# Output products of a diffusion block: from float32 pairs to scaled float16 pairs

## The chip, the cores and the metric

One core of one Trainium2 chip runs the whole kernel in one launch. The metric is the device time of one execution in microseconds. Before the change three runs took 2703.93, 2701.36 and 2702.88 us (median 2702.88).

## What is computed

The reference is one block of a diffusion transformer over 2048 tokens of width 1024, in float32. The input projection and the gates are followed by a Fourier mixer (512 channels) and by a neighbourhood attention (8 heads of 64) side by side. Their outputs are merged, projected and added to the stream, and an MLP follows. What the change touches is the merge:

```python
def gated_merge(h, y_four, y_attn, w_gate, w_fo, w_ao, w_o):
    gates = jax.nn.sigmoid(h @ w_gate)
    g_f, g_a = jnp.split(gates, N_BRANCHES, axis=-1)
    merged = g_f * (y_four @ w_fo) + g_a * (y_attn @ w_ao)
    return merged @ w_o
...
    x = x + g1 * mixed
```

Here `y_attn` is 2048x512, `w_ao` 512x1024, `w_o` 1024x1024.

## The kernel before

Precise products are made from pairs. A float32 tile is split into a high part and the rest (`split_on`, L85: ACT copies the high part, L87, another engine subtracts, L90), and `mm3` (L76) issues three matmuls per pair of operands, high x high, high x low, low x high, all on line L82. Some products take float16 pairs whose operands are scaled beforehand (the projections `ps_*`, the MLP products `pm` and `p`). Others, among them the two of this change, take pairs of type float32r, a 4-byte type.

The stages, in order of time in the profiled execution:

- To 850 us: norm, modulation and projections in pairs of weight units. The last pair is two gate units, g6 and g7 (`run_pair`, called for n = 7). A unit of 24 matmuls fills one bank `ps_g` of a PSUM pool of four, and ACT takes the sigmoid of it (`put_T`, L509) into one of two tiles `ot`, which SP stores to gT. Beside these units the generator `fourier_prep` loads four tables `tw` of 1 MB through the two buffers of the tag "wst" and splits them. `turn` and `pace` set how many of its steps are taken between two steps of the gate units.
- 850 to 902 us: the Fourier mixer. `channel_dft` evacuates `pc` into pairs gH/gL and eH/eL (ACT, then DVE), `seq_dft` (L954) and `seq_dft64` (L969) make products `psq` of them with the tables and store the results (tile A) to yF and y64.
- 902 to about 1222 us: attention, 64 blocks. In each, PE makes scores `sc`, DVE a masked maximum (L1258), ACT the exponential (L1262), PE transposes `tp`, ACT and DVE split them into pH/pL (L1274, L1279), and PE multiplies by the values, `pv`. The generator `beside_attention` fills the gaps of PE: first the Fourier output product (`merge_fourier`, tile pmf, into mF), then the loading of w_attn_out (tiles wao to waH/waL, both steps on POOL, L89 and L90), then the first merge tile, `attn_out(0)`.
- `attn_out(t)` (L1305) handles 256 tokens: it loads and splits the attention output (yaH, yaL), and for each of 8 column groups m PE makes 12 matmuls of 128x256 into `pua`. DVE multiplies by the gate ga (L1328), adds the gated Fourier part ft (L1329), and ACT and DVE split the sum into mH/mL. ga, gf and ft are loaded for two groups at a time into two buffers each; ft is multiplied by gf on L1321.
- About 1190 to 1247 us: `attn_out(1)`, and between its groups the eight row blocks of w_out are loaded (`stage_wo`, tile wou), multiplied by the gain row g1r (L1476) and split.
- 1247 to 1506 us, the merge loop: for each of eight tiles of 256 tokens, two `out_proj` (L1400), each two banks `po` of 24 matmuls of 128x512, evacuated on DVE with the addition of the stream (L1411), then `attn_out(t + 2)` and `norm_T(t)` (transposes `tpb`). `pua` and `po` rotate through one PSUM pool of four banks, "mm".
- From 1506 us: the MLP, with PE as the bound.

A list scheduler of the framework orders each engine's instructions from the program; the waits follow from tiles, buffers and queues.

## Time and profile before

| | |
|---|---|
| median of three runs | 2702.88 us |
| the profiled execution's own time | 2706.24 us |
| its span | 2704.4 us |
| PE busy | 2563.6 us, 95% of the span |
| PE weight loads (beside the matmuls) | 1564.8 us, 58% |
| DVE, ACT, POOL busy | 1813.9, 1169.9, 462.6 us |
| mean granted PE clock | 0.979 |

The busy share of an engine is an average over stages with different limits. What one stage is worth is read from its own stretch of the chain of waits, which follows the last instruction back to what released it, step by step. A matmul's own duration overlaps the next one's: what it costs in a row of matmuls is the distance from one to the next, which a piece of the chain gives as its time divided by its count.

### The profile page before, as it was taken

To read this page: it belongs to the slowest core of one execution; us is meant where nothing else is said; L and a number is where in the kernel's file an instruction comes from. 1 tells how busy PE (TensorE), PEld (TensorE's weight loads), DVE (VectorE), ACT (ScalarE), POOL (GpSimd) and SP (SyncE) were. 2 spreads that over 40 slices of the span, in tenths; PEclk is the share of its full clock that TensorE was granted. 3 is DMA by queue.
4 is the path that set the end of the run, shared out by engine and by line. 5 is a ranking of instruction groups with operands and counts; after the bars stand their busy time and mean duration, and the time that the engine had idled before them with its cause. 6 is when DMAs were issued, how large, how long until landed. Compare 5 with 4: busy or idle time off the path is not lost.

```text
span 2704.4 us, 42578 instructions
## 1 busy us (share of the span) xinstructions
PE 2563.6 (95%) x15825; PEld 1564.8 (58%) x15825; DVE 1813.9 (67%) x3636; ACT 1169.9 (43%) x2097; POOL 462.6 (17%) x702
## 2 busy tenths in 40 slices
PE   7899988898999799998999789999999999999999
PEld 5445656766656678887888434444444444444444
DVE  7746975567562588897766596888876743636367
ACT  5623325544231578883444373636352332314050
POOL 1201211012233454531000012121210100000000
PEclk9999989998999899998999899999999999999999
DMA  8576789766353744556667677777766633333334
GB/s 265 148 223 199 216 235 295 259 217 202 102 171 95 191 131 139 143 178 218 218 208 266 216 226 262 230 261 241 252 224 227 209 94 109 94 110 93 112 101 154
DMA packets 344232, 509.36 MB, mean 188 GB/s; under 512 B 48369, under 2 KB 210377, under 8 KB 339673
## 3 DMA queue, kind: packets, MB, share of 16 engines
q1 hardware_dynamic: 294249, 398.11, 47.4%
q0 software_dynamic: 28544, 73.39, 8.0%
q10 hardware_dynamic: 21232, 35.15, 4.0%
q8 instruction: 124, 2.03, 0.3%
q14 instruction: 83, 0.68, 0.1%
HBM read 361.72 MB, written 145.84 MB: 188 GB/s over the span
## 4 chain that ended last, share of the span: by engine, by line
PE 71%; DMA 11%; DVE 10%; ACT 3%; issue 2%; POOL 1%; SPq 1%; ACTq 0%; DVEq 0%; POOLq 0%
PE p L82 21%; PE pm L82 19%; PE ps_g L82 8%; PE po L82 7%; DMA w12m<-in_w_mlp 4%; PE pua L82 3%; PE tp L1271 2%; PE ps_k L82 2%; PE pmf L1209 2%; PE pv L1285 2%; DMA raw<-in_w_mlp 1%; PE sc L1249 1%; PE ps_f L82 1%; DMA vF<-vo_v 1%; DVE wo L381 1%
## 5 line engine op out<-in xcount | busy, mean ns | idle before, releaser
L82 PE MATMUL pm<-hc,wb 128*128 128x512 f16 x2688 | 587.1, 381 | 21.5 <-DMA hc<-hcd 12.0
L82 PE MATMUL p<-wb,a 128*128 128x512 f16 x2688 | 581.8, 379 | 2.7 <-DVE X L1666 1.6
L82 PEld LDWEIGHTS <-wb 128*128 128x128 f16 x2688 | 263.9, 98 | 343.2 <-issue 29.5
L82 PEld LDWEIGHTS <-a 128*128 128x128 f16 x2688 | 262.9, 98 | 320.3 <-issue 3.4
L82 PE MATMUL ps_g<-hx,w_g 128*128 128x512 f16 x1536 | 344.3, 382 | 1.2 <-ACT ot_f L509 1.2
L1546 DVE TENSOR_TENSOR X<-X,p 128x512 f32<-128x512 f32 x280 | 183.8, 682 | 176.1 <-PE p L82 155.3
L82 PEld LDWEIGHTS <-hx 128*128 128x128 f16 x2304 | 228.7, 100 | 49.2 <-issue 9.9
L82 PEld LDWEIGHTS <-w_g 128*128 128x128 f16 x1536 | 151.5, 99 | 173.4 <-issue 6.1
L1546 DVE TENSOR_TENSOR u<-pm,u 128x512 f32<-128x512 f32 x128 | 87.5, 688 | 90.5 <-PE pm L82 88.9
L1037 POOL DMA_DIRECT2D bt<-tT x264 | 132.4, 508 | 77.0 <-DVE ri L1278 58.0
L1258 DVE CUSTOM_DVE_ANT_0 s<-sc,bt,qsc 128x736 f32<-128x736 f32 (+5 forms) x128 | 111.1, 868 | 41.3 <-PE sc L1252 37.8
L380 ACT ACTIVATE wo<-ws,msc 128x512 f16<-128x512 f32 x96 | 68.9, 718 | 152.2 <-DVE ws L423 119.6
L1550 ACT ACTIVATE p<-pm 128x512 f32<-128x512 f32 x32 | 18.9, 589 | 239.4 <-PE pm L82 239.2
L509 ACT ACTIVATE ot_g<-ps_g,usc_g 128x512 f32<-128x512 f32 x64 | 43.7, 684 | 174.8 <-PE ps_g L82 162.4
L1279 DVE SCALAR_TENSOR_TENSOR pL<-tp,pH 128x640 f16<-128x640 f32 (+1 forms) x128 | 112.1, 876 | 6.6 <-ACT pH L1274 6.3
L380 ACT ACTIVATE wo<-raw,msc 128x512 f16<-128x512 f32 x128 | 87.8, 710 | 66.1 <-issue 25.5
L1680 POOL DMA_DIRECT2D xr<-x1d x32 | 17.3, 539 | 570.3 <-DVE X L1546 562.1
L1262 ACT ACTIVATE s<-s,m 128x736 f32<-128x736 f32 (+5 forms) x128 | 104.4, 816 | 13.1 <-DVE m L1258 12.4
L82 PE MATMUL po<-wouH,mH 128*128 128x512 f32 x256 | 101.0, 398 | 7.1 <-DVE ga L1328 7.1
L1271 PE MATMUL tp<-ident,s 128*128 128x128 f32 x704 | 105.0, 283 | 2.1 <-ACT s L1262 2.0
L82 PE MATMUL po<-wouL,mH 128*128 128x512 f32 x256 | 100.2, 393 | 0.0
L82 PE MATMUL po<-wouH,mL 128*128 128x512 f32 x256 | 100.2, 393 | 0.0
(503 smaller groups left out, 4741.4 us busy)
## 6 DMA issues: line engine op xcount, KB each, us to landing
wb<-w1d SPq DMA_DIRECT2D x224, 256.0 KB
wb<-w2d SPq DMA_DIRECT2D x224, 256.0 KB
w12m<-in_w_mlp SPq DMA_DIRECT2D x32, 1024.0 KB
raw<-in_w_mlp ACTq DMA_DIRECT2D x24, 1024.0 KB
w1d<-wo POOLq DMA_DIRECT2D x84, 256.0 KB, 3.8
w2d<-wo POOLq DMA_DIRECT2D x84, 256.0 KB, 3.9
gT<-ot_g SPq DMA_DIRECT2D x64, 256.0 KB
hc<-hcd SPq DMA_DIRECT2D x14, 1024.0 KB
```

What stands on the lines that cost most here:

```text
L82: last_mm[0] = pe.matmul(ps, l, r, start=(start and i == 0), stop=(stop and i == n - 1))
L380: act.activation(hi, src, AF.Copy, scale=scale)
L381: dve.scalar_tensor_tensor(out=lo, in0=src, scalar=scale, in1=hi, op0=ALU.mult, op1=ALU.subtract)
L509: act.activation(o, ps, func, scale=scale)
L1037: load_(t[i * 16:(i + 1) * 16, :, off + j0 * w:off + (j0 + 8) * w], raw(tT[ct], (2 * hp * 15 + dr) * w, [[120 * w, 16], [15 * w, 2], [1, 8 ...
L1209: pe.matmul(ps, l, r, start=(i == 0), stop=(i == len(prods) - 1))
L1258: tail["dve"] = dve.tensor_tensor_reduce(out=s[:, :n], in0=sc, in1=bias, op0=ALU.add, op1=ALU.min, scale=qsc[:, 4:5], scalar=3.0e38, accum ...
L1262: tail["act"] = act.activation(s[:, :n], s[:, :n], AF.Exp, bias=m1[:, 0:1], scale=-1.0, accum_out=m1[:, 1:2])
L1271: tail["pe"] = pe.transpose(tp[:, i * 128:(i + 1) * 128], s[:, o:o + 128], ident)
L1279: tail["dve"] = dve.scalar_tensor_tensor(out=pL[:, :c], in0=tp[:, :c], scalar=PTOP, in1=pH[:, :c], op0=ALU.mult, op1=ALU.subtract)
L1285: tail["pe"] = pe.matmul(pv, p_[:nk, i * 128:(i + 1) * 128], vv[:nk, h2 * 128 + o:h2 * 128 + o + 64], start=(j == 0 and i == 0), stop=(j = ...
L1546: last["dve"] = dve.tensor_tensor(out=o, in0=x, in1=y, op=op)
```

## The change

The four operands of the two products (waH/waL, yaH/yaL, mH/mL, woH/woL) become float16 pairs. So that their values fit this type, they are scaled by powers of two, and the evacuations multiply by the inverse. What the scales need is computed on the chip:

- In `fourier_prep`, after each table, two 1 MB parts of w_attn_out (2), w_out (4) and w_fourier_out (2) are loaded through the same two "wst" buffers, and ACT squares each with a sum per row (wn). The pace beside the last pair is 3 in place of 2.
- After each result of `seq_dft` and `seq_dft64` DVE takes its largest magnitude (ymax).
- A new function `merge_scales`, called ahead of attention, forms the scales mgs from these, through PE and POOL, and scales the gain row g1r.
- Each part of w_attn_out is first scaled, on POOL. The attention output is left in its own scale (another constant, 1.0 / PTOP).
- The evacuations of `pua` and `po` and the addition of ft take a scale: scalar_tensor_tensor in place of tensor_tensor.

```diff
@@ run_pair
-        pace[0] = (0, 3, 2)[min(n, 2)]
+        pace[0] = 3 if n == len(seq) - 1 else (0, 3, 2)[min(n, 2)]
@@ fourier_prep, after the split of table i
+            for j in (2 * i, 2 * i + 1):
+                w, k = ((a["w_attn_out"][0], j), (a["w_out"][0], j - 2), (a["w_fourier_out"][0], j - 6))[(j >= 2) + (j >= 6)]
+                tn = pa.tile([128, 2, D], F32, tag="wst", name=f"wn{j}", bufs=2)
+                sp.dma_start(tn, w[k * 256:(k + 1) * 256, :].rearrange("(k p) n -> p k n", p=128))
+                tn = tn.rearrange("p k n -> p (k n)")
+                act.activation(tn, tn, AF.Square, accum_out=wn[:, j:j + 1])
                 yield
@@ seq_dft (seq_dft64 alike, with 4 rows)
             act.dma_start(yF[p][i % 2][:, (i // 2) * 512:(i // 2 + 1) * 512], o)
+            dve.tensor_reduce(out=ymax[:, 4 * p + i:4 * p + i + 1], in_=o, axis=AX.X, op=ALU.max, apply_absolute_value=True)
+    def merge_scales():
+        dve.tensor_reduce(out=ymax[:, 10:11], in_=view(col, 1, [[2, 2]]), axis=AX.X, op=ALU.max, apply_absolute_value=True)
+        dve.tensor_reduce(out=ymax[:68, 11:12], in_=col[:68, 5:6], axis=AX.X, op=ALU.max, apply_absolute_value=True)
+        y, b = mgs[:, 4:5], mgs[:, 5:6]
+        dve.tensor_reduce(out=y, in_=ymax, axis=AX.X, op=ALU.max)
+        ps = smp.tile([128, 512], F32, tag="sm", name="pym")
+        pe.transpose(ps[0:1, :128], y, ident)
+        dve.tensor_reduce(out=mgs[0:1, 6:7], in_=ps[0:1, :128], axis=AX.X, op=ALU.max)
+        ps = smp.tile([128, 512], F32, tag="sm", name="pyb")
+        pe.matmul(ps[:, 0:1], ones[0:1, :], mgs[0:1, 6:7], start=True, stop=True)
+        pe.matmul(ps[:, 8:16], ones, wn, start=True, stop=True)
+        dve.tensor_copy(y, ps[:, 0:1])
+        ws = mgs[:, 7:10]
+        for i, (j, n) in enumerate(((0, 2), (2, 4), (6, 2))):
+            dve.tensor_reduce(out=ws[:, i:i + 1], in_=ps[:, 8 + j:8 + j + n], axis=AX.X, op=ALU.add)
+        pool.tensor_tensor(ws, ws, half[:, 0:3], op=ALU.pow)
...
+        dve.tensor_reduce(out=y, in_=g1r, axis=AX.X, op=ALU.max, apply_absolute_value=True)
...
+        dve.tensor_scalar(out=g1r, in0=g1r, scalar1=y, scalar2=None, op0=ALU.mult)
@@ attn_out
-        yH, yL = (pm.tile([128, 4, W], F32R, tag="y" + o, name=f"ya{o}{t}") for o in "HL")
+        yH, yL = (pm.tile([128, 4, W], F16, tag="y" + o, name=f"ya{o}{t}") for o in "HL")
...
-            dve.tensor_tensor(out=gt, in0=ps, in1=gt, op=ALU.mult)
-            dve.tensor_tensor(out=gt, in0=gt, in1=ft[:, m % 2], op=ALU.add)
-            split_on(dve, mH[:, m, :], mL[:, m, :], gt)
+            dve.scalar_tensor_tensor(out=gt, in0=ps, scalar=mgs[:, 1:2], in1=gt, op0=ALU.mult, op1=ALU.mult)
+            dve.scalar_tensor_tensor(out=gt, in0=ft[:, m % 2], scalar=mgs[:, 2:3], in1=gt, op0=ALU.mult, op1=ALU.add)
+            act.activation(mH[:, m, :], gt, AF.Copy)
+            dve.tensor_tensor(out=mL[:, m, :], in0=gt, in1=mH[:, m, :], op=ALU.subtract)
@@ load_wa, in place of load_rows_of
+            pool.tensor_scalar(wt, wt, mgs[:, 0:1], None, op0=ALU.mult)
+            pool.tensor_copy(wa[0][:, k, :], wt)
+            pool.tensor_tensor(wa[1][:, k, :], wt, wa[0][:, k, :], op=ALU.subtract)
@@ out_proj
-            dve.tensor_tensor(out=x1[:, ns], in0=ps, in1=x1[:, ns], op=ALU.add)
+            dve.scalar_tensor_tensor(out=x1[:, ns], in0=ps, scalar=mgs[:, 3:4], in1=x1[:, ns], op0=ALU.mult, op1=ALU.add)
```

What the change moves stands in the order of the engines' instructions (line of the respective file, operation, outputs<-inputs, size). First ACT beside the last gate pair: ot_g are the evacuations of the gate units, tH the casts of the tables, wn the squares. Before:

```order
L87 ACTIVATE tH3_8784<-tw3_8786 128x512 x4
L509 ACTIVATE ot_g61_0_8503<-ps_g61_0_8478,usc_g6_7660 128x512
L509 ACTIVATE ot_g61_1_8533<-ps_g61_1_8508,usc_g6_7660 128x512
L509 ACTIVATE ot_g71_0_8567<-ps_g71_0_8542,usc_g7_7664 128x512
L509 ACTIVATE ot_g71_1_8597<-ps_g71_1_8572,usc_g7_7664 128x512
L509 ACTIVATE ot_g62_0_8627<-ps_g62_0_8602,usc_g6_7660 128x512
L509 ACTIVATE ot_g62_1_8657<-ps_g62_1_8632,usc_g6_7660 128x512
```

and now:

```order
L515 ACTIVATE ot_g71_0_8578<-ps_g71_0_8553,usc_g7_7667 128x512
L882 ACTIVATE wn5_8774,wn_140<-wn5_8774 128x2048
L515 ACTIVATE ot_g71_1_8608<-ps_g71_1_8583,usc_g7_7667 128x512
L87 ACTIVATE tH3_8805<-tw3_8807 128x512 x4
L882 ACTIVATE wn6_8873,wn_140<-wn6_8873 128x2048
L515 ACTIVATE ot_g62_0_8641<-ps_g62_0_8616,usc_g6_7663 128x512
L882 ACTIVATE wn7_8876,wn_140<-wn7_8876 128x2048
L515 ACTIVATE ot_g62_1_8672<-ps_g62_1_8647,usc_g6_7663 128x512
```

The casts of the last table have moved behind four more evacuations of the pair's units and six of the eight squares stand between these evacuations; the last, wn7, stands ahead of that of the tenth unit (unit 9, counted from 0). Second, DVE at the end of the Fourier stage and the start of attention (A64 is the last Fourier result, s0 the first masked scores). Before:

```order
L949 SCALAR_TENSOR_TENSOR A64_0_9230<-alt_8887,col_141,psq64_0_9217 4x512
L1258 ISA s0_9358,m10_0_0_9409<-sc0_0_0_9404,bt0_9249,qsc_136 128x520
L1258 ISA m10_0_0_9409 128x1
L1258 ISA s1_9359,m11_0_0_9417<-sc1_0_0_9412,bt0_9249,qsc_136 128x520
L1258 ISA m11_0_0_9417 128x1
```

and now:

```order
L962 SCALAR_TENSOR_TENSOR A64_0_9266<-alt_8914,col_144,psq64_0_9253 4x512
L992 TENSOR_REDUCE ymax_141<-A64_0_9266 4x1
L992 TENSOR_REDUCE ymax_141<-A64_2_9283 4x1
L1000 TENSOR_REDUCE mgs_142<-ymax_141 128x1
L1003 TENSOR_REDUCE mgs_142<-pym_9290 1x1
L1007 COPY mgs_142<-pyb_9293 128x1
L1010 TENSOR_REDUCE mgs_142<-pyb_9293 128x1 x3
L1311 ISA s0_9428,m10_0_0_9479<-sc0_0_0_9474,bt0_9319,qsc_136 128x520
L1311 ISA m10_0_0_9479 128x1
L1311 ISA s1_9429,m11_0_0_9487<-sc1_0_0_9482,bt0_9319,qsc_136 128x520
```

Eight instructions, two of which read results of PE, have come ahead of the first scores; the rest of `merge_scales` stands between the first blocks. Third, POOL late in attention, where w_attn_out is split, with the product ft of `attn_out(0)` behind it. Before:

```order
L89 CAST waH_14326<-wao0_14328 128x1024
L89 CAST waH_14326<-wao1_14332 128x1024
L90 TENSOR_TENSOR waL_14327<-wao0_14328,waH_14326 128x1024
L90 TENSOR_TENSOR waL_14327<-wao1_14332,waH_14326 128x1024
L89 CAST waH_14326<-wao2_14336 128x1024
L89 CAST waH_14326<-wao3_14340 128x1024
L90 TENSOR_TENSOR waL_14327<-wao2_14336,waH_14326 128x1024
L90 TENSOR_TENSOR waL_14327<-wao3_14340,waH_14326 128x1024
L1321 TENSOR_TENSOR ft0_0_14661<-ft0_0_14661,gf0_0_14660 128x512
```

and now:

```order
L1392 TENSOR_SCALAR wao0_14398<-wao0_14398,mgs_142 128x1024
L1392 TENSOR_SCALAR wao1_14403<-wao1_14403,mgs_142 128x1024
L1393 CAST waH_14396<-wao0_14398 128x1024
L1393 CAST waH_14396<-wao1_14403 128x1024
L1394 TENSOR_TENSOR waL_14397<-wao0_14398,waH_14396 128x1024
L1394 TENSOR_TENSOR waL_14397<-wao1_14403,waH_14396 128x1024
L1392 TENSOR_SCALAR wao2_14408<-wao2_14408,mgs_142 128x1024
L1392 TENSOR_SCALAR wao3_14413<-wao3_14413,mgs_142 128x1024
L1393 CAST waH_14396<-wao2_14408 128x1024
```

Two scalings have come ahead of each pair of casts.

## Rows read from the trace of the kernel before

**Rows 1.** The page: the span, PE's line of part 1 (busy us, share of the span, instructions; PEld is the weight load), and the second line of part 4 (shares of the chain that ended last, by line).

```profile
span 2704.4 us, 42578 instructions
...
PE 2563.6 (95%) x15825; PEld 1564.8 (58%) x15825; DVE 1813.9 (67%) x3636; ACT 1169.9 (43%) x2097; POOL 462.6 (17%) x702
...
PE p L82 21%; PE pm L82 19%; PE ps_g L82 8%; PE po L82 7%; DMA w12m<-in_w_mlp 4%; PE pua L82 3%; PE tp L1271 2%; PE ps_k L82 2%; PE pmf L1209 2%; PE pv L1285 2%; DMA raw<-in_w_mlp 1%; PE sc L1249 1%; PE ps_f L82 1%; DMA vF<-vo_v 1%; DVE wo L381 1%
```

**Rows 2.** The chain of waits in order of time, from the first output projection to the third tile of the merge loop: start us, us, what.

```profile
1247.62 24.29 PE po L82 x96
...
1292.70 14.30 PE po L82 x63
1307.00 11.51 PE pua L82 x96
...
1319.38 7.54 PE po L82 x33
...
1342.08 11.51 PE pua L82 x96
```

**Rows 3.** The same view in the key projections (ps_k, 128x256) and in the first MLP product (pm, 128x512), both with float16 operands.

```profile
662.32 2.62 PE ps_k L82 x24
...
1682.87 72.52 PE pm L82 x336
```

**Rows 4.** Instructions of the tiles po and pua by shape (duration ns min/median/max, first and last start us), and part 5 of the page for the weight loads of pm (count, busy us, mean ns).

```profile
L82 PEld LDWEIGHTS po<-wouH,mH x256: 187/188/330, 1247.6 to 1504.9; 128*128 128x128 f32 x128
...
L82 PEld LDWEIGHTS pua<-yaH,waH x256: 186/192/330, 1186.3 to 1458.2; 128*128 128x128 f32 x128
...
L82 PEld LDWEIGHTS <-wb 128*128 128x128 f16 x2688 | 263.9, 98 | 343.2 <-issue 29.5
```

**Rows 5.** Busy time by stretch: us, PE busy (instructions), PEld, DVE, ACT, POOL, then granted PE clock, DMA share, GB/s. First one tile of the merge loop, then the staging of w_out before it; then the merge loop with the instructions of po alone and of pua alone (PE, PEld, DVE).

```profile
1307.00:1342.00 35.00, 35.00 (x209) 31.15 (x209) 24.04 (x50) 14.69 (x26) 1.48 (x2) 1.00 0.66 218
1222.00:1247.60 25.60, 15.37 (x129) 14.81 (x128) 18.19 (x25) 7.50 (x13) 5.04 (x2) 0.80 0.64 213
...
1272.00:1506.00 234.00, 156.22 (x672) 125.12 (x672) 19.17 (x28) 1.00 0.65 221
...
1272.00:1506.00 234.00, 69.77 (x576) 69.45 (x574) 19.21 (x48) 1.00 0.65 221
```

**Rows 6.** The last gate pair and the loads beside it. The timeline of ACT, SP and DVE (start us, us, engine line op out<-in xcount [idle before <-releaser]), busy time by stretch as above, and the squares of L334 by shape.

```profile
818.53 0.69 ACT L509 ACTIVATE ot_g<-ps_g,usc_g 128x512 f32<-128x512 f32 x1 [4.49 <-PE ps_g L82]
...
820.00:850.00 30.00, 30.00 (x144) 14.06 (x142) 0.00 (x0) 3.83 (x6) 0.42 (x1) 1.00 0.15 54
...
L334 ACT ACTIVATE w12m<-w12m x16: 1907/1911/1912, 420.6 to 491.6; 128x2048 f32<-128x2048 f32 x16
...
748.67 6.78 SPq L867 DMA_DIRECT2D tw<-in_seq  x2
...
859.32 0.32 SPq L807 DMA_DIRECT2D X<-fT  x1
...
864.40 0.69 DVE L818 TENSOR_TENSOR s<-X 128x511 f32<-128x511 f32 x1 [3.04 <-DMA X<-fT]
```

**Rows 7.** The Fourier stage: the only reductions of 128x512 in it by shape, and DVE's timeline.

```profile
L827 DVE TENSOR_REDUCE spc<-fold x4: 675/678/680, 785.2 to 870.0; 128x2 f32<-128x512 f32 x4
...
874.28 0.42 DVE L90 TENSOR_TENSOR gL<-pc,gH 128x256 fp32r<-128x256 f32 x1 [1.53 <-ACT gH L87]
...
878.78 0.42 DVE L90 TENSOR_TENSOR gL<-pc,gH 128x256 fp32r<-128x256 f32 x1 [2.96 <-ACT gH L87]
```

**Rows 8.** The start of attention: DVE's timeline, the chain in order of time, and the powers of L165 on POOL by shape.

```profile
902.93 0.76 DVE L1258 CUSTOM_DVE_ANT_0 s<-sc,bt,qsc 128x520 f32<-128x520 f32 x1 [2.60 <-PE sc L1252]
...
907.63 0.16 DVE L1278 RECIPROCAL ri<-m 128x1 f32<-128x1 f32 x1
...
911.79 1.21 DVE L1153 TENSOR_TENSOR ws<-wf,wm 128x1024 f32<-128x1024 f32 x1
...
925.66 11.16 DMA Q<-qH
...
L165 POOL TENSOR_TENSOR rs<-ms,mhalf x16: 543/577/1537, 12.3 to 119.7; 128x1 f32<-128x1 f32 x16
```

**Rows 9.** POOL's timeline where w_attn_out is split, beside the last blocks of attention; then POOL's and DVE's timeline at the staging of w_out.

```profile
1163.41 4.69 POOL L90 TENSOR_TENSOR waL<-wao,waH 128x1024 fp32r<-128x1024 f32 x2
1169.36 1.04 POOL L89 CAST waH<-wao 128x1024 fp32r<-128x1024 f32 x1 [1.26 <-DMA wao<-in_w_attn_out]
1172.72 1.04 POOL L89 CAST waH<-wao 128x1024 fp32r<-128x1024 f32 x1 [2.33 <-DMA wao<-in_w_attn_out]
...
1184.82 1.28 POOL L1321 TENSOR_TENSOR ft<-ft,gf 128x512 f32<-128x512 f32 x1 [6.41 <-DMA ft<-mF]
...
1235.40 5.04 POOL L90 TENSOR_TENSOR wouL<-wou,wouH 128x1024 fp32r<-128x1024 f32 x2 [27.24 <-ACT mH L87]
...
1235.50 2.66 DVE L1329 TENSOR_TENSOR ga<-ga,ft 128x256 f32<-128x256 f32 x1
```

**Rows 10.** DVE's timeline at the fifth evacuation of pua in a tile of the merge loop, and two forms of 128x256 by shape: the two-tensor form of L1328, the three-operand form of L270.

```profile
1318.35 0.76 DVE L1328 TENSOR_TENSOR ga<-pua,ga 128x256 f32<-128x256 f32 x2 [1.71 <-DMA ga<-gT]
...
L1328 DVE TENSOR_TENSOR ga<-pua,ga x64: 406/425/427, 1191.4 to 1461.0; 128x256 f32<-128x256 f32 x64
...
L270 DVE SCALAR_TENSOR_TENSOR aaccc<-awtc,sil,aaccc x48: 470/474/478, 136.7 to 203.2; 128x256 f32<-128x256 f32 x48
```

More of the change, by code (lines that the diff above doesn't have):

```diff
@@ L129, in dit_block @@
     pool.memset(mhalf, -0.5)
-    half = cp.tile([128, 1], F32, tag="half", name="half")
+    half = cp.tile([128, 4], F32, tag="half", name="half")
     pool.memset(half, 0.5)
@@ L151, in dit_block @@
     msc = cp.tile([128, 6], F32, tag="msc", name="msc")
+    wn = cp.tile([128, 8], F32, tag="wn", name="wn")
+    ymax = cp.tile([128, 12], F32, tag="ymax", name="ymax")
+    mgs = cp.tile([128, 12], F32, tag="mgs", name="mgs")
     hsc = cp.tile([128, 4], F32, tag="hsc", name="hsc")
@@ L481, in load_unit @@
         act.activation(sq, wt.rearrange("p k n -> p (k n)"), AF.Square, accum_out=u[:, 5:6])
-        pool.tensor_tensor(u[:, 5:6], u[:, 5:6], half, op=ALU.pow)
+        pool.tensor_tensor(u[:, 5:6], u[:, 5:6], half[:, 0:1], op=ALU.pow)
         yield
@@ L977, in seq_dft64 @@
             act.dma_start(y64[:, (i // 2) * 512:(i // 2 + 1) * 512], o)
+            dve.tensor_reduce(out=ymax[:4, 8 + i // 2:9 + i // 2], in_=o, axis=AX.X, op=ALU.max, apply_absolute_value=True)
+    def merge_scales():
[14 more added lines that the diff above has]
+        pool.tensor_tensor(ws, ws, half[:, 0:3], op=ALU.pow)
+        dve.scalar_tensor_tensor(out=b, in0=ws[:, 0:1], scalar=PTOP * VTOP * 512 ** 0.5, in1=vsc[:, 2:3], op0=ALU.mult, op1=ALU.mult)
+        dve.scalar_tensor_tensor(out=y, in0=y, scalar=2 * 512 ** 0.5, in1=ws[:, 2:3], op0=ALU.mult, op1=ALU.mult)
+        dve.tensor_tensor(out=b, in0=b, in1=y, op=ALU.add)
+        power_of_two(b, HTOP, 1.0e-9)
+        dve.reciprocal(mgs[:, 2:3], b)
+        power_of_two(ws[:, 0:1], HTOP, 1.0e-9)
+        dve.reciprocal(mgs[:, 0:1], ws[:, 0:1])
+        dve.scalar_tensor_tensor(out=mgs[:, 1:2], in0=ws[:, 0:1], scalar=PTOP, in1=vsc[:, 2:3], op0=ALU.mult, op1=ALU.mult)
+        dve.tensor_tensor(out=mgs[:, 1:2], in0=mgs[:, 1:2], in1=mgs[:, 2:3], op=ALU.mult)
+        dve.tensor_reduce(out=y, in_=g1r, axis=AX.X, op=ALU.max, apply_absolute_value=True)
+        o = ws[:, 1:2]
+        dve.tensor_tensor(out=o, in0=o, in1=y, op=ALU.mult)
+        power_of_two(o, HTOP, 1.0e-9)
+        dve.tensor_tensor(out=mgs[:, 3:4], in0=o, in1=b, op=ALU.mult)
+        dve.reciprocal(y, o)
+        dve.tensor_scalar(out=g1r, in0=g1r, scalar1=y, scalar2=None, op0=ALU.mult)
@@ L979, in dit_block @@
+    pool.memset(ymax, 0.0)
     channel_dft(0)
@@ L1308, in attn_out @@
         (fetch if t == 0 else sp.dma_start)(yt, yA[:, :, ts].rearrange("k p t -> p k t"))
-        yH, yL = (pm.tile([128, 4, W], F32R, tag="y" + o, name=f"ya{o}{t}") for o in "HL")
+        yH, yL = (pm.tile([128, 4, W], F16, tag="y" + o, name=f"ya{o}{t}") for o in "HL")
         eng = dve if t else pool
-        split_on(eng, yH, yL, yt)
-        mH, mL = (m_pool.tile([128, 8, W], F32R, tag="m" + o, name=f"m{o}{t}", bufs=2 if t else 1) for o in "HL")
+        act.activation(yH, yt, AF.Copy)
+        eng.tensor_tensor(out=yL, in0=yt, in1=yH, op=ALU.subtract)
+        mH, mL = (m_pool.tile([128, 8, W], F16, tag="m" + o, name=f"m{o}{t}", bufs=2 if t else 1) for o in "HL")
         merged[t] = (mH, mL)
@@ L1343, in beside_attention @@
         pm = sbuf("mga")
-        wa = [pm.tile([128, 4, D], F32R, tag="wa" + o, name="wa" + o) for o in "HL"]
-        load_rows_of(pm, a["w_attn_out"][0], wa[0], wa[1], 4, "wao")
+        wa = [pm.tile([128, 4, D], F16, tag="wa" + o, name="wa" + o) for o in "HL"]
+        load_wa()
         while n < order.index((3, 0, 3)) + 3:
@@ L1390, in dit_block @@
     pg = sbuf("mgb", "right")
-    wo = [pg.tile([128, 8, D], F32R, tag="wo" + o, name="wou" + o) for o in "HL"]
+    wo = [pg.tile([128, 8, D], F16, tag="wo" + o, name="wou" + o) for o in "HL"]
     normed, x1s, x1r = {}, [], iter(range(0, S, 128))
@@ L1476, in dit_block @@
         dve.tensor_tensor(out=wt, in0=wt, in1=g1r, op=ALU.mult)
-        split_on((pool, dve)[k % 2], wo[0][:, k, :], wo[1][:, k, :], wt)
+        act.activation(wo[0][:, k, :], wt, AF.Copy)
+        (pool, dve)[k % 2].tensor_tensor(out=wo[1][:, k, :], in0=wt, in1=wo[0][:, k, :], op=ALU.subtract)
     for _ in attn:
```

15 lines of the change are left out of this document (8 added, 7 removed).

## The prediction

> **What bounds the kernel now.** I read the busy shares and the chain of waits first. PE is busy 2563.6 us of a span of 2704.4 us (95%), and in the chain that ended last the two products that the change touches hold 7% (po, the output projection) and 3% (pua, the attention projection) [rows 1]. The chain in order of time shows how they stand there: from 1247.6 to 1506 us it is one unbroken run of PE pieces, a tile's 96 pua, then its 96 po in two pieces (33 and 63) around eight transposes, and a tile comes every 1342.08 - 1307.00 = 35.08 us [rows 2]. In such a tile PE is busy 35.00 of 35.00 us at full granted clock (1.00, the 2.4 GHz level), DVE 24.0, ACT 14.7, the DMA engines 0.66 [rows 5]. So in this stretch a matmul made shorter is time gained, unless something that now has a few us of room takes its place. The whole run (2706.24 us) stands 3.4 us above the median of the runs shown (2702.88 us). I sum against the former and take 3.4 off at the end. A change under 0.2% (5.4 us) can't be told from none.
>
> **What the faster format gives.** The number of matmuls stays (three per product, before and after). Before, 63 po matmuls of 512 columns take 14.30 us, 0.227 us each, and 96 pua of 256 columns 11.51 us, 0.120 us each [rows 2]. What the same shapes cost with float16 pairs is in the same trace: 336 pm matmuls of 512 columns in 72.52 us, 0.2158 each, and 24 ps_k of 256 columns in 2.62 us, 0.1092 each [rows 3]. That is 0.0112 us less per po and 0.0107 per pua. The stretch from 1272 holds 672 po and 576 pua [rows 5]: 672 x 0.0112 = 7.5 us and 576 x 0.0107 = 6.2 us. The first 96 po (24.29 us, 0.253 each [rows 2]) give 0.5 of their 1.1, since they begin when the last staged weights are there. The other 192 pua lie beside attention and the staging of w_out, where PE is busy 15.4 of 25.6 us [rows 5]; I count 1.0 of their 2.1. Sum of gains 15.2 us; the bounds are 13.7 and 16.8.
>
> A weight load of float32 type takes 188 ns in po and 192 in pua, of float16 98 [rows 4]. These loads run beside the matmuls: 0.227 and 0.120 us from one matmul to the next is no sum of load and matmul, so I count nothing for them. The Trainium skill (TensorE: Matmul & The Clock Gate, Weight-path perf modes) says that the fast weight load is on for 128 weights of a type that isn't FP32. The two durations agree with it. If the loads stood in the path, 1536 x 90 ns = 138 us would be gained by it; the distances between matmuls say that they don't.
>
> **Eight more loads and squares beside the last gate pair.** There PE works without a gap (30.00 of 30.00 us), with the DMA engines at 0.15 [rows 6], and ACT evacuates a unit of 24 matmuls every 4.49 + 0.69 = 5.18 us [rows 6]. Eight squares of 1.91 us [rows 6] fit into the idle 4.49 us. What may hurt is their place in ACT's order, where a square that waits for its load holds the evacuations behind it. The twelve loads (four tables, eight weights) share two buffers, six rounds each, from 748.67 on [rows 6]; a load of 1 MB took 5.1 us (X, issued at 859.32, used at 864.40) [rows 6]. The last load, wn7, waits for the split of the last table, which stands behind the evacuation of unit 7 (two units before the one at 818.53, so 808.2). Walking the order with these prices it lands between 818 and 824. Its square stands ahead of the evacuation of unit 9 (818.53), whose bank PE wants for unit 13, three units later, at 834.0; less square and evacuation that leaves until 831.4, 7 us of room. I take 0, up to 21 (below).
>
> **Maxima in the Fourier stage.** Ten reductions, eight of 0.68 us [rows 7], stand on DVE between the subtractions that the next matmuls wait for. DVE is idle 1.5 and 3.0 us before those, waiting for ACT [rows 7]; by the order at most two maxima stand together ahead of one (1.4 us). I take 1.5 us, between 0 (all in the idle time) and 4 (5.4 us of reductions less one such gap).
>
> **The scales at the start of attention.** Ahead of the first softmax instruction DVE now has two small maxima, a transposition of the maximum on PE, a broadcast, four small reductions and a copy; it was idle 2.60 us there, waiting for PE [rows 8]. A dozen instructions of 0.15 us [rows 8] and two trips over PE make about 3 us more. Some twenty tiny instructions (3 us), POOL's power (0.58 us), and a maximum and a scaling of the 128x1024 gain row (1.21 us each, as a 128x1024 operation took [rows 8]) follow among the first blocks, 6 us of DVE. Behind them on DVE stand the maxima and divisions of the blocks, for which PE and ACT wait; behind the power on POOL stand its transfers of the bias. What covers it is a wait for data: the chain here is Q<-qH for 11.16 us until 936.8 [rows 8], and that does not start later. I take 2.5 us of the 9, bounds 0 and 9.
>
> **Four more scalings on POOL.** Each tile of w_attn_out is now scaled on POOL before the two steps that were there: 1.04 us for a cast, 2.35 for a subtraction (4.69 for two) [rows 9], so 4.2 to 9.4 us for four. POOL waits 1.26 and 2.33 us for the loads and then 6.41 us for ft [rows 9], ahead of the first pua. I take 1 us, bounds 0 and 3.
>
> At the staging of w_out a row shows what POOL can cost DVE: while POOL subtracts for 5.04 us, DVE's addition of two 128x256 operands takes 2.66 us [rows 9], against 0.425 for a multiplication of that size [rows 10]. The Trainium skill (SBUF — State Buffer, "SBUF: two separate sides") says that a DVE operation with two inputs in SBUF and a POOL operation lock each other out of a shared port pair for a whole instruction, which agrees with this row. By that rule the four scalings could hold DVE for up to 9.4 us more if such instructions stood beside them. The order puts softmax instructions beside them, each with one operand in PSUM, so I add nothing.
>
> The scaling of the output of attention only changes its constant: nothing.
>
> **Evacuations with a scale, and the room in the loop.** A scalar_tensor_tensor of 128x256 takes 474 ns where the two-tensor form takes 425 [rows 10]; 16 per tile are 0.8 us of DVE, which has 11 us idle in a tile [rows 5]. Only the last evacuations are on the chain: 0.5. But room between PE and the gates is small: the fifth evacuation of pua starts at 1318.35 after a wait of 1.71 us for ga [rows 10], needs 0.42 for its tile, and po starts at 1319.38 in the bank that it frees [rows 2]: 0.6 us left. The pua phase shrinks by 1.0 us, so where ga is late PE stops for part of that. ga waits for a buffer freed by DVE's own work in the tile before, and moves up only in part. I take 1.5 us over the six tiles, bounds 0 and 13 (the whole gain of this stretch).
>
> **Sum.** -15.2 + 0 + 1.5 + 2.5 + 1 + 0.5 + 1.5 = -8.2 us: 2698.0 us for the profiled run, 2694.7 against the median.
>
> **Rivals.**
> A, the room goes: gates or buffers set the pace of the merge loop. For it speak the waits for ga [rows 10]; against it DVE's 11 and ACT's 20 idle us per tile. The gain of 13.7 in the loop falls to 3 or less, the time comes to about 2702 to 2706. No change. Chance 0.15.
> B, slower: the evacuation of gates waits behind a square that waits for its weights. Decides when wn7 lands after 831. If each 1 MB round takes 4.7 us longer than 5.1 (six rounds in each buffer, 28 us in all), it lands at 852, and PE stands for 21 us in a stretch in which it now never stops: 2694.7 + 21 = 2716; half of that gives 2705. For it speaks that stores of gates share SP's queue and that two buffers leave one load ahead; against it the DMA share of 0.15 [rows 6]. Chance 0.11 beyond 2708, and 0.05 of a stall that only eats the gain.
> C, the scales at the start of attention and POOL's scalings are not covered: 9 + 3 in place of 3.5, so 2703. For it speaks DVE at the head of every block; against it the 11 us wait for Q. Chance 0.09.
> D, the format does not change the pitch of these matmuls (it is bound by reading what both kinds read): the gain is 0, the additions remain, 2710. Against it are the float16 rows of equal shape [rows 3]. Chance 0.02.
>
> **How the numbers follow.** My forecast has 0.58, so that faster by over 5.4 us (below 2697.5) has 0.60 with the good tails of the rivals, slower by over 5.4 (above 2708.3) 0.12, and no change 0.28. The range goes from the gain of 16.8 with nothing lost (2686) to 2709: past A and C, leaving out most of B.
>
> **What would show it.** Right: po pieces of 63 in 13.6 us, pua pieces of 96 in 10.5 us, and a period of 33.0 to 33.4 us; PE without gaps from 750 to 850; the first pieces of attention a few us late and the Q wait shorter by as much; MLP unchanged but earlier. Wrong: pua waits in PE's rows ahead of po (A); gaps before ps_g, with ACT waiting for wn (B); the first projection of the merge loop starting more than 8 us after its old time, less what changed before (C).

## The result and the profile after

The changed kernel takes 2683.8 us (median of 11 runs, 2680.0 to 2690.8), the kernel before beside it 2701.9 us (11 runs, 2690.0 to 2704.3). The ratio is 0.9941, with a 95% interval of 0.9929 to 0.9952: 16 us faster, 13 to 19. A second series gave 0.9935 (0.9922 to 0.9949). The forecast was 8 us faster, with 2686 as the lowest time, so the direction was right, the size was half of what came, and the time lies 2.2 us below that lowest one. One of these is the base: the forecast started from a median of 2702.88 us, and eleven runs give 2701.9.

The page of the profiled execution (2680.04 us) answers to [rows 1]: the span, PE's line of part 1, the chain by line.

```profile
span 2678.3 us, 42654 instructions
...
PE 2540.9 (95%) x15830; PEld 1473.7 (55%) x15830; DVE 1825.6 (68%) x3672; ACT 1183.4 (44%) x2113; POOL 480.2 (18%) x708
...
PE p L82 21%; PE pm L82 19%; PE ps_g L82 8%; PE po L82 6%; DMA w12m<-in_w_mlp 4%; PE pua L82 3%; PE ps_k L82 2%; PE pmf L1262 2%; PE tp L1324 2%; SPq L188 1%; PE pv L1338 1%; PE ps_f L82 1%; DMA raw<-in_w_mlp 1%; PE sc L1302 1%; PE ps_v L82 1%
```

PE is busy 22.7 us less. The span itself is 26 us shorter, more than the runs say, and a part of that is no effect of the change: the profiled execution of before stands 4.4 us above its kernel's median (2706.2 against 2701.9), that of the changed kernel 3.8 below its own, and the two profiles are already 7.8 us apart at the end of the key projections, where little of the change has run. So the comparison goes by stretches between events of PE, read from the first and last start of each tile's matmuls by shape. Each column is one stretch in us, each row the profile of one kernel:

```
                       last key   last gate   first pmf   last pmf    third pua  first pm   first p
                       to last    to first    to last     to third    to first   to first   to last
                       gate       pmf         pmf         pua tile    pm         p          p
before                 88.8       118.3       188.8       115.7       233.9      102.6      1090.7
before, again          88.8       120.4       188.8       116.4       234.0      103.2      1090.6
e1_types               88.8       118.9       188.7       113.1       220.1      102.6      1090.6
e2_additions           88.8       118.2       187.4       120.7       234.0      102.6      1090.7
changed                88.9       116.3       187.4       117.3       220.0      100.8      1090.1
changed, again         88.8       120.5       187.4       118.1       220.0      100.9      1090.1
e3_no_squares          88.8       120.2       187.4       119.0       220.0      100.8      1090.2
e4_no_scales           88.9       114.1       188.5       117.9       220.0      101.4      1090.1
e5_wou_dve             88.9       114.8       187.3       117.6       220.1      102.4      1090.6
e6_wa_act              88.9       116.0       187.4       131.8       220.0      103.3      1090.2
e7_no_wa_scale         88.8       118.7       187.3       109.2       220.5      101.6      1090.1
e8_wa_dve              88.8       116.1       187.4       125.0       220.6      103.2      1090.5
e9_both                88.8       113.7       187.4       112.0       220.1      100.8      1090.2
e10_four_bufs          88.8       116.5       187.4       117.0       220.1      102.5      1090.7
e11_bufs_pool          88.8       116.4       187.4       112.9       220.6      102.7      1090.6
e12_bufs_dve           88.8       116.4       187.5       115.7       220.7      102.0      1090.7
```

With the means of the two profiles of either kernel, changed less before: 0.0, -0.9, -1.4, +1.6, -13.9, -2.1, -0.6, in sum -17.3 us, which agrees with the ratio. The merge loop carries most of it. Where a program was profiled twice, each stretch repeats within 0.8 us, except that from the last gate to the first pmf; the other rows rest on one profile each. The merge loop's chain of waits (start us, us, what), which answers to [rows 2]:

```profile
1251.63 10.74 PE po L82 x49
1262.37 10.48 PE pua L82 x96
...
1273.72 7.55 PE po L82 x35
...
1282.15 13.17 PE po L82 x61
1295.32 10.48 PE pua L82 x96
```

61 po take 13.17 us, 0.216 each, 96 pua 10.48 us, 0.109 each: the prices of [rows 3]. The period is 1295.32 - 1262.37 = 32.95 us against 35.08. Busy time of one tile of that loop and then of the last gate pair, each row with the columns of [rows 5]:

```profile
1295.40:1328.30 32.90, 32.90 (x210) 20.52 (x208) 25.08 (x50) 14.62 (x26) 1.48 (x2) 1.00 0.67 227
...
752.50:841.40 88.90, 88.90 (x419) 40.98 (x418) 29.79 (x52) 35.95 (x53) 18.11 (x16) 1.00 0.65 216
```

PE has no gap in either. DVE needs 1.0 us more per tile (25.08 against 24.04) and still has 7.8 us idle. In the second row the DMA share has risen from 0.36 to 0.65 and ACT from 21 to 36 us against the same stretch before, and PE doesn't stop.

### The profile page after: what moved, and what is told of

It reads as the page before. It is cut to its first block, busy times and chain, and to the rows that moved or that the text cites. A ratio compares the mean times of both kernels' runs of the same rounds, so it can differ in the third digit from the quotient of the medians.

```text
span 2678.3 us, 42654 instructions
## 1 busy us (share of the span) xinstructions
PE 2540.9 (95%) x15830; PEld 1473.7 (55%) x15830; DVE 1825.6 (68%) x3672; ACT 1183.4 (44%) x2113; POOL 480.2 (18%) x708
## 4 chain that ended last, share of the span: by engine, by line
PE 69%; DMA 11%; DVE 10%; issue 2%; ACT 2%; POOL 2%; SPq 2%; ACTq 0%; DVEq 0%; POOLq 0%
PE p L82 21%; PE pm L82 19%; PE ps_g L82 8%; PE po L82 6%; DMA w12m<-in_w_mlp 4%; PE pua L82 3%; PE ps_k L82 2%; PE pmf L1262 2%; PE tp L1324 2%; SPq L188 1%; PE pv L1338 1%; PE ps_f L82 1%; DMA raw<-in_w_mlp 1%; PE sc L1302 1%; PE ps_v L82 1%
## 5 line engine op out<-in xcount | busy, mean ns | idle before, releaser
L1738 POOL DMA_DIRECT2D xr<-x1d x32 | 17.3, 541 | 570.8 <-DVE X L1604 562.0
L82 PE MATMUL po<-wouH,mH 128*128 128x512 f16 x256 | 96.8, 382 | 9.2 <-DVE ga L1382 9.2
L82 PE MATMUL po<-wouL,mH 128*128 128x512 f16 x256 | 97.8, 382 | 3.2 <-POOL wouL L1535 3.2
L387 DVE SCALAR_TENSOR_TENSOR wo<-raw,msc,wo 128x512 f16<-128x512 f32 x128 | 94.4, 745 | 5.8 <-ACT wo L386 5.8
```

The lines of the kernel that those rows point to most:

```text
L82: last_mm[0] = pe.matmul(ps, l, r, start=(start and i == 0), stop=(stop and i == n - 1))
L387: dve.scalar_tensor_tensor(out=lo, in0=src, scalar=scale, in1=hi, op0=ALU.mult, op1=ALU.subtract)
```

## Experiments

**The format alone, the additions alone.** `e1_types` is the kernel before with the four types changed and nothing else:

```diff
-            split_on(dve, mH[:, m, :], mL[:, m, :], gt)       # float32r tiles
+            act.activation(mH[:, m, :], gt, AF.Copy)          # float16 tiles; wa, ya, wo alike
+            dve.tensor_tensor(out=mL[:, m, :], in0=gt, in1=mH[:, m, :], op=ALU.subtract)
```

> The kernel before with only the types changed: the four operands of the two products are float16 pairs, nothing is scaled, and no sum of squares, maximum or scale is computed (the scaling is what is left out). Theory 1 (the format is the gain, the additions are covered): 13 to 16 us faster than before, the period of the merge loop at 33.0 to 33.4 us. Theory 2 (part of the gain comes from what the additions do to the start of attention): 10 to 12 us faster, the stretch from the first scores to the first pmf as long as before, 65 us.

Measured: ratio 0.9947 (0.9932 to 0.9962), 14 us faster. `e2_additions` is the changed kernel with these four types put back to float32r.

> The changed kernel with all its additions (loads, squares, maxima, scales, scaled evacuations), but the operands of the two products of type float32r as before. Theory 1: the additions are covered, 0 to 3 us slower than before; by the terms of the prediction it would be 7 us slower. Theory 2: 3 to 6 us faster than before, gained between the first scores and the first pmf (63 us or less in place of 65).

Measured: 1.0013 (1.0002 to 1.0024), 3.5 us slower (0.5 to 6.5). That is just above theory 1 (0 to 3) and under the 7 of the prediction's terms; theory 2 falls. The table says where: the types give 13.9 us in the loop and about 3 before it, the additions cost about 4.6 between the last pmf and the third pua tile (116.0 to 120.7; 113.1 to 117.7 with float16) and give back 1.4 in the stretch of pmf. What in the type makes a matmul shorter isn't parted: its operands have two bytes in place of four, and the weight loads fell as well (31.15 us in a tile before [rows 5], 20.52 now).

**Two profiles of each program.**

> The kernel before, unchanged, for what two executions of one program differ by. If the 7.7 us by which the changed kernel's profile leads at the first channel transform (849.4 to 841.4 us), before most of what was changed, are scatter of the executions, this profile reaches that place at another time than 849 too, by 3 us or more, with the differences in the stretch from 400 to 560 us; if they belong to the changed kernel, it is there at 848 to 851 us.

Measured: 1.0002 (0.9992 to 1.0013). Its last gate matmul starts at 844.1 us, not at 849.1; of these 5.0 us half is there at 560 us, as expected, and half comes in the key projections. The lead of 7.7 us in the first pair of profiles is thus scatter for the most part, and it is about what the two profiled executions differ by from the medians of their kernels (4.4 and 3.8 us).

> The changed kernel, unchanged, for its scatter and a second profile: the stretches from the last key projection on should repeat within 2.5 us each (88.9 us to the last gate matmul, 53.2 to the first score, 63.1 to the first pmf, 187.4 to the last, 117.3 to the third pua tile, 220.1 to the first pm, 100.8 to the first p), and the start of the last gate pair lies between 716 and 724 us.

Measured: 0.9935 (0.9922 to 0.9949). All stretches repeat within 0.8 us but one: from the last gate to the first pmf it is 120.5 us in place of 116.3, more than the 2.5 expected. That stretch scatters between 113.7 and 120.5 us over all kernels. Busy time by stretch shows what goes with it, in the 20 us that begin 100 us after the last gate matmul starts, first the changed kernel, then its second profile (columns of [rows 5]):

```profile
941.40:961.40 20.00, 18.29 (x214) 13.78 (x215) 15.01 (x33) 14.65 (x34) 7.13 (x15) 1.00 0.13 30
```

```profile
941.70:961.70 20.00, 17.01 (x184) 11.81 (x181) 13.92 (x28) 12.23 (x30) 4.19 (x9) 0.83 0.06 11
```

At a granted clock of 0.83 (a mix of the 2.4 and the 1.2 GHz level) PE did 184 instructions there, at 1.00 (the 2.4 GHz level) it did 214. Over all 16 profiles the same 20 us part them without an exception: the seven at 0.80 or 0.83 (before twice, e1, e2, e3, e7, the changed kernel's second) have 118.2 to 120.5 us from the last gate to the first pmf, the nine at 0.90 to 1.00 have 113.7 to 116.5. What lowers the clock in one execution and not in the other stays open.

**Are the squares and the scales covered?** `e3_no_squares` takes the loads and squares out of `fourier_prep`, sets wn to a constant and the pace back to 2.

> The changed kernel without the eight loads and squares of weights (a constant takes the place of the sums, the pace beside the last pair is 2 again). Theory 1: they are covered but for 1 us, so the time of the changed kernel within 2 us, ratio to before 0.993 to 0.995. Rival (the loads change what comes later, since they end the load of the tables otherwise): 3 us or more from the changed kernel, to either side, and PE idle between 720 and 850 us as before (0) rather than 1.0 us.

Measured: 0.9944 (0.9928 to 0.9960), the same as the changed kernel; its last gate pair takes 88.8 us. `e4_no_scales` drops the maxima and the call (`seq_dft64` alike):

```diff
-            dve.tensor_reduce(out=ymax[:, 4 * p + i:4 * p + i + 1], in_=o, ...)
...
-    pool.memset(ymax, 0.0)
+    pool.memset(mgs, 1.0)
...
-    merge_scales()
```

> The changed kernel without the maxima of the Fourier results and without the scales (constants of 1 take their place, the gain row isn't scaled); loads, squares and scaled evacuations stay. If these steps cost what the prediction said, the stretch from the last gate matmul to the first pmf is 4 us shorter than in the changed kernel (116.3 us there, 118.3 and 120.4 in two profiles of before). If they are covered (theory 1), it is 116 to 120 us, and the time that of the changed kernel within 2 us. From the first to the last pmf: 187.4 us if the scaled loading of w_attn_out orders this stretch, 188.8 if the scales do. The order of DVE and ACT behind the last projection is that of the changed kernel, so the stretch from the first pm to the first p should take 100.8 us.

Measured: 0.9943 (0.9931 to 0.9956), the same again. The stretch to the first pmf is 114.1 us, against 113.7 to 116.5 (mean 115.8) in the eight profiles with the scales at as high a clock, so a cost of about 2 us can't be excluded from one profile, but none shows in the times. The stretch of pmf is 188.5 us as before the change: its 1.4 us go with the scales. On PE the order of instructions there is one and the same in the twelve profiles with 187.3 to 187.5 us, and another in the four with 188.5 to 188.8 (before twice, e1, e4). So these 1.4 us go with the order, which the additions happen to move; that the order alone makes them wasn't tried.

**What costs 4.6 us late in attention.** Two places were suspected: POOL's scalings of w_attn_out, and POOL's subtractions of w_out. `e5_wou_dve` moves the latter:

```diff
-        (pool, dve)[k % 2].tensor_tensor(out=wo[1][:, k, :], in0=wt, in1=wo[0][:, k, :], op=ALU.subtract)
+        dve.tensor_tensor(out=wo[1][:, k, :], in0=wt, in1=wo[0][:, k, :], op=ALU.subtract)
```

> The changed kernel with all eight subtractions of w_out on DVE (four were on POOL). Theory (DVE and POOL hold each other up where both read two operands in SBUF): the last POOL subtraction goes from the chain, the first 96 po take 22 to 23.5 us in place of 26.1, DVE's subtractions and products there take 0.4 to 1.25 us each and none 2 to 5, and the kernel is 2 to 4 us faster than the changed one. Rival (POOL is late because its input is late): the wait of 3.2 us ahead of the second projection stays, now for DVE. Behind the last projection DVE and ACT stand in the order of the kernel with only the types changed, so the stretch from the first pm to the first p should be 102.6 us again, 1.8 us more than in the changed kernel.

Measured: 0.9943 (0.9929 to 0.9956), no gain. PE's waits from the first po to the third pua tile (engine line waited for: us in total, times, longest), first the changed kernel, then e5:

```profile
PE po L82 <- DVE ga L1382: 9.2, 1, 9.2
PE po L82 <- POOL wouL L1535: 3.2, 1, 3.2
```

```profile
PE po L82 <- DVE ga L1382: 12.0, 1, 12.0
```

The wait for POOL went as forecast, the first 96 po fell from 26.1 to 23.3 us, and the wait for DVE ahead of them grew by as much. DVE's operations there took 0.4 to 1.25 us and none 2 to 5, as the theory said, but the 2 to 4 us didn't come. The chain shows what DVE itself waited for, first in e5, then in `e12_bufs_dve` below, each time just ahead of the first 96 po:

```profile
1225.91 9.17 DMA wou<-in_w_out
```

```profile
1229.25 9.14 DMA wou<-in_w_out
```

What stands there is a load of w_out, so moving the subtraction only moved the wait. The third forecast held: 102.4 us from the first pm to the first p.

`e6_wa_act` and `e8_wa_dve` move the four scalings, `e7_no_wa_scale` leaves them out, `e9_both` is e7 with the edit of e5:

```diff
-            pool.tensor_scalar(wt, wt, mgs[:, 0:1], None, op0=ALU.mult)
+            act.activation(wt, wt, AF.Copy, scale=mgs[:, 0:1])                                   # e6
+            dve.tensor_scalar(out=wt, in0=wt, scalar1=mgs[:, 0:1], scalar2=None, op0=ALU.mult)   # e8
```

> The changed kernel with the four scalings of w_attn_out on ACT in place of POOL. If they are what makes the stretch from the last pmf to the third pua tile 4 to 5 us longer in the kernels with the additions (117.3 us against 113.2 with the types alone), it is 113 to 115 us here. If the subtractions of w_out on POOL are, it stays at 117 to 119. From the first pm to the first p 102.6 us, by the order of DVE and ACT there.

Measured: 0.9994 (0.9986 to 1.0002), the whole gain gone, 131.8 us. The expectation was wrong.

> The changed kernel with the four scalings of w_attn_out on DVE, where one of this size took 0.75 us. If only their price on POOL counts, the stretch from the last pmf to the third pua tile is 114 to 116 us. If a scaling that waits for its load holds the attention blocks behind it, as on ACT (waits of 6.7 and 2.1 us for the loads, 131.8 us in all), it is 125 us or more and the kernel 8 us or more slower than the changed one.

Measured: 0.9972 (0.9956 to 0.9988), 125.0 us: the second case. The timelines of ACT in e6 and of DVE in e8 show why:

```profile
1175.16 1.15 ACT L1392 ACTIVATE wao<-wao,mgs 128x1024 f32<-128x1024 f32 x1 [6.67 <-DMA wao<-in_w_attn_out]
1178.35 1.15 ACT L1392 ACTIVATE wao<-wao,mgs 128x1024 f32<-128x1024 f32 x1 [2.05 <-DMA wao<-in_w_attn_out]
```

```profile
1178.36 0.75 DVE L1392 TENSOR_SCALAR wao<-wao,mgs 128x1024 f32<-128x1024 f32 x1 [7.44 <-DMA wao<-in_w_attn_out]
```

An engine that every attention block needs stands still for a load that waits for a buffer.

> The changed kernel without the four scalings of w_attn_out on POOL (left out, so this operand keeps its own size). If these four (2.85 us each, 11.4 in all) delay the first pua and so the end of attention, the stretch from the last pmf to the third pua tile is 113 to 115 us in place of 117.3 and 118.1, PE doesn't wait for yaL, and the time is 2 to 4 us below the changed kernel's. Rival (the scaled evacuations and the later order of the pua matmuls make the stretch longer): it stays at 117 to 118. From the first pm to the first p 100.8 us, by the order there.

Measured: 0.9913 (0.9892 to 0.9934), some 7 us below the changed kernel, with intervals that just touch, and 109.2 us, less than expected. So leaving out the four scalings shortens this stretch by 8.5 us in these profiles (and by 5.6 from e5 to e9, where the subtractions of w_out stand on DVE). How they cost it, POOL's timeline and SP's waits of the changed kernel show (the waits from the last pmf on for 50 us):

```profile
1150.77 5.68 POOL L1392 TENSOR_SCALAR wao<-wao,mgs 128x1024 f32<-128x1024 f32 x2
1156.41 2.02 POOL L1393 CAST waH<-wao 128x1024 f16<-128x1024 f32 x2
1158.41 4.23 POOL L1394 TENSOR_TENSOR waL<-wao,waH 128x1024 f16<-128x1024 f32 x2
1164.00 2.85 POOL L1392 TENSOR_SCALAR wao<-wao,mgs 128x1024 f32<-128x1024 f32 x1 [1.37 <-DMA wao<-in_w_attn_out]
1167.08 2.85 POOL L1392 TENSOR_SCALAR wao<-wao,mgs 128x1024 f32<-128x1024 f32 x1 [0.24 <-DMA wao<-in_w_attn_out]
1169.88 2.02 POOL L1393 CAST waH<-wao 128x1024 f16<-128x1024 f32 x2
1171.86 4.24 POOL L1394 TENSOR_TENSOR waL<-wao,waH 128x1024 f16<-128x1024 f32 x2
1183.55 2.12 POOL L1365 TENSOR_TENSOR yaL<-yat,yaH 128x1024 f16<-128x1024 f32 x1 [7.45 <-ACT yaH L1364]
```

```profile
SPq L1050 <- POOL waL L1394: 22.0, 3, 14.3
```

```profile
1174.03 0.38 SPq L1050 DMA_DIRECT2D yat<-yA  x1
```

Part 3 of w_attn_out can't be loaded before POOL has subtracted part 1, since "wst" has two buffers, and the attention output yat takes a buffer of the same tag: its load is issued at 1174.03, when POOL is done with the third part, 28.9 us after the last pmf. All later loads of SP stand behind it, and yaL, for which the first tile of pua waits, begins 38.5 us after the last pmf. The same waits and the same load in the kernel before (1178.28, 22.1 us after its last pmf; yaL at 30.1), and the load in e7 (21.8 us; yaL at 29.8):

```profile
SPq L997 <- POOL waL L90: 10.2, 3, 8.1
```

```profile
1178.28 0.53 SPq L997 DMA_DIRECT2D yat<-yA  x1
```

```profile
1167.52 0.53 SPq L1050 DMA_DIRECT2D yat<-yA  x1
```

So the scalings delay the load of yat by 7 us and the first pua by 8. That is still no account of the whole stretch: e1 begins its first pua as early as e7 (29.5 us after the last pmf) and needs 113.1 us. Where the other 4 us come from wasn't tried.

> The changed kernel without the four scalings of w_attn_out (left out) and with all subtractions of w_out on DVE. With the subtractions alone moved, the first 96 po took 23.3 us in place of 26.1, but began 3 us later, no gain. If the late first pua was what took that gain, the two together give 110 to 112 us from the last pmf to the third pua tile. If the staging of w_out on DVE is the bound there, it is 113 to 115 as without the scalings alone.

Measured: 0.9914 (0.9891 to 0.9937) and 112.0 us: nothing beyond e7. The number falls into the first case, its meaning, a gain from the two edits together, didn't come.

**Four buffers.** `e10_four_bufs` and `e11_bufs_pool` give the parts of w_attn_out a tag of their own; e10 has their scalings on DVE, e11 on POOL:

```diff
-            wt = pm.tile([128, D], F32, tag="wst", name=f"wao{k}", bufs=2)
+            wt = pm.tile([128, D], F32, tag="wst4", name=f"wao{k}", bufs=4)
```

> The changed kernel with four buffers for the parts of w_attn_out (all four loads start at once) and their scalings on DVE. With two buffers DVE waited 7.4 us for the third load, which waited for POOL, and attention behind it. If that wait was the loss, DVE now waits under 2 us, the stretch from the last pmf to the third pua tile is 110 to 114 us (117.3 and 118.1 in the changed kernel, 125.0 with DVE and two buffers) and the kernel is 3 to 6 us faster than the changed one, ratio to before 0.9915 to 0.993. Rival (the loads themselves come too late for a scaling at that place in DVE's order): a wait of over 5 us ahead of the first scaling, and no gain.

Measured: 0.9948 (0.9936 to 0.9960), no gain over the changed kernel, 117.0 us (125.0 with two buffers). DVE no longer waits, so the expected loss is gone, but its order has the four scalings late and POOL's first cast starts at 1168.7 us, 22 us after the last pmf. Whether that takes the gain isn't shown: yaL begins 32.9 us after the last pmf here, earlier than in the changed kernel.

> The changed kernel with four buffers for the parts of w_attn_out, scaled on POOL as in the changed kernel. If POOL's own time for the four parts (23.9 us of work) sets when the first pua starts, this differs from the changed kernel by under 2 us: 116 to 118 us from the last pmf to the third pua tile. If its waits for the loads do (1.4 and 0.2 us there), it is no more than 2 us shorter too; if it is 113 us or less, neither is the cause and the order is.

Measured: 0.9930 (0.9917 to 0.9943) and 112.9 us, with POOL's scalings as long as before. SP waits for POOL no more, and yat is loaded 18.7 us after the last pmf:

```profile
1166.91 0.59 SPq L1050 DMA_DIRECT2D yat<-yA  x1
```

yaL begins 25.7 us after the last pmf. So about five of the 8.5 us go without POOL's time getting any shorter. But POOL's order changed as well, ft and yaL now stand between its steps for w_attn_out,

```profile
1172.67 1.27 POOL L1375 TENSOR_TENSOR ft<-ft,gf 128x512 f32<-128x512 f32 x1 [5.48 <-DMA ft<-mF]
1173.91 2.13 POOL L1365 TENSOR_TENSOR yaL<-yat,yaH 128x1024 f16<-128x1024 f32 x1
...
1177.23 1.04 POOL L1393 CAST waH<-wao 128x1024 f16<-128x1024 f32 x1
```

and the expectation had named the order as the cause of such a result. How much is the buffer and how much the order isn't parted. In the whole, e11 is at best 1 to 3 us faster than the changed kernel, and the intervals overlap: its stretch from the first pm to the first p is 1.9 us longer. `e12_bufs_dve` adds the edit of e5.

> The changed kernel with four buffers for the parts of w_attn_out, their scalings on POOL, and all subtractions of w_out on DVE. With four buffers SP no longer waits for POOL (22.0 us of waits in the changed kernel, the longest 14.3) and the first yat load is issued 18.7 us after the last pmf in place of 28.9. If POOL's late merge work (ft, yaL, the subtractions of w_out) is what holds the rest, the stretch from the last pmf to the third pua tile is 109 to 111 us here (112.9 with four buffers alone, 109.2 without the scalings), the third pua tile isn't split by waits, and the ratio to before is 0.991 to 0.993. If the staging on DVE is the bound, it is 112 to 114 and the time that of four buffers alone.

Measured: 0.9934 (0.9917 to 0.9951), 115.7 us, no better than e11 and beyond both ranges. The load of w_out shown at e5 stands ahead of the first po here too; in e11 and e10 a load of gates does:

```profile
1229.95 6.88 DMA ga<-gT
```

```profile
1232.46 7.00 DMA ga<-gT
```

So ahead of the first po stand loads that SP issues, whichever engine subtracts; no run was made on those loads. No version with all its scales is clearly faster than the changed kernel.

## Why the prediction was right in sign and half in size

- **The format: right.** The forecast was 13.7 us in the loop from 672 po and 576 pua; the loop shrank by 13.9 us, at the prices of the float16 rows. Before the loop the forecast was 1.5; e1 shows 2.9 (116.0 to 113.1), in one profile. Rival D (no gain by the type) is out.
- **Squares beside the gates: right.** 88.9 us against 88.8. The last square and the evacuations behind it, in ACT's timeline:

```profile
815.67 1.91 ACT L882 ACTIVATE wn<-wn 128x2048 f32<-128x2048 f32 x1 [2.34 <-DMA wn<-in_w_fourier_out]
...
817.58 1.24 ACT L515 ACTIVATE ot_g<-ps_g,usc_g 128x512 f32<-128x512 f32 x2
821.11 0.69 ACT L515 ACTIVATE ot_g<-ps_g,usc_g 128x512 f32<-128x512 f32 x1 [2.29 <-PE ps_g L82]
```

  With the 7.7 us that this execution is ahead, 815.67 is 823.4 of the old time: inside the forecast of 818 to 824. Eight evacuations came 1 to 7 us after their last matmul in place of 0.1; that of unit 9, at 817.58, came 6.9 us late, 7.8 us ahead of unit 13, the next to take its bank (826.04), and PE saw none of it. Rival B is out.
- **The step that failed: "The scales at the start of attention" and "Maxima in the Fourier stage", +2.5 and +1.5.** They cost nothing that can be measured: among the seven profiles at the lower clock the stretch from the last gate to the first pmf has a mean of 119.4 us in the four with them and 119.2 in the three without, and at the higher clock it is 115.8 in eight with them and 114.1 in e4. The forecast had named the cover, the wait for Q, and then took a quarter of 9 us all the same. In the changed kernel's first profile that wait is a piece of 3.09 us in place of 11.16 [rows 8]:

```profile
923.41 3.09 DMA Q<-qH
```

  Rival C is out at this place; its other half, the scalings on POOL, came true at two to three times its price.
- **"The room in the loop" and the scaled evacuations, +1.5 and +0.5: nothing.** The loop is 220.0 us with scaled evacuations and 220.1 without (e1). L1382 takes 483 ns (425 before [rows 10]), and it fits. Rival A is out.
- **"Four more scalings on POOL", +1, bounds 0 and 3: far too small.** They cost 8.5 us by e7 and 5.6 by e5 and e9; all additions together make this stretch 4.6 us longer. Two errors: the price, 2.85 us each where the bounds from a cast and a subtraction were 1.04 and 2.35; and the place, since the working looked at POOL's idle time ahead of ft, not at the load of yat, which waits on SP for a buffer that POOL frees (issued 28.9 us after the last pmf in place of 22.1).
- **Not in the forecast: the order.** 1.4 us in the stretch of pmf, 2.1 from the first pm to the first p and 0.6 in the MLP. Behind the last projection DVE and ACT stand in one order in six profiles (100.8 to 101.6 us: the changed kernel twice, e3, e4, e7, e9) and in three others in the remaining ten (102.0 to 103.3). For e4 to e7 this was on record before they ran, and came within 0.8 us. It goes with the order; which exchange of instructions makes the 2 us wasn't tried.

The parts missed by 5 us (the stretch to the first pmf), 2 (the loop) and 4 (the order) on the side of a gain, and by 2 on the other (the stretch with POOL): 9 us, the distance between -8.2 and -17.3. Of the 5 us, 4 are the costs that didn't come and 1 goes with the clock, since one of the changed kernel's two profiles was at the higher one there and neither of the kernel before. The range was too narrow at its lower end because it left no room for gains that the sum did not contain, such as a moved order. The forecast was nearer than its terms earned: the cost on POOL that it missed took back a part of the gains that it missed.

## What to carry to other kernels

Price a faster operand type by the distance between matmuls of the same shape in the same trace; that term held to 0.2 us of 14 here. Cost an added step not only where its engine is idle but by the buffers that it keeps and by the queue that waits for them: 11.4 us on a nearly idle engine cost 6 to 8 here, and on a busy engine, waiting for the same buffer, 7 to 14 more. A change in one stage can move a scheduler's order in stages that it doesn't touch (1 to 2 us each went with that here), and 4 us of one stretch went with the granted clock of the execution; two profiles of each program, compared at the same clock, are the least that such a comparison needs.
